# A two-layer decoder trunk in which an accumulating DMA, and no compute engine, forms the low halves of split weights

## The chip, the core and the metric

The kernel runs on one core of a Trainium2 chip. Its engines are TensorE (PE in the profile, with its weight loads as PEld), VectorE (DVE), ScalarE (ACT), GpSimd (POOL) and SyncE (SP), which here only issues DMAs. SBUF is the core's working memory, PSUM takes the matmuls' results, and 16 DMA engines move data between DRAM and SBUF or within SBUF. The metric is the device time of one execution in microseconds (us), as the median of several runs.

## What is computed

A sequence of 16 meta tokens and 512 real ones passes through differential attention, a feed-forward network (FFN), an attention in which every query keeps only its best keys, and a second FFN. All arithmetic is float32. The parts that matter here are the products with weights:

```python
def conv_ffn(h, w_up, conv_w, conv_b, w_down):
    u = h @ w_up
    ...
    return (jax.nn.silu(g) * val) @ w_down

q, k, v = jnp.split(h @ w_qkv, 3, axis=-1)          # layer 0
...
return o.reshape(B, T, DA_HEADS * 2 * DA_HEAD_DIM) @ w_o
q, k, v, qi, ki, wi = jnp.split(h @ w_in, DSA_SPLITS, axis=-1)   # layer 1
...
return o.reshape(B, T, DSA_QKV) @ w_o
```

## The kernel before, in words

Each float32 operand of a matmul is split into a rounded high part and a low part that holds the rest, both in the type float32r. A product is then three matmuls: high by high, high by low, low by high. Activations lie in SBUF, feature by token, 528 tokens wide (512 or 516 in the last layer's FFN).

Weights come in *slabs*: 1024 rows (896 for the first two thirds of the FFN's second matrix) by 128 columns, as one tile of 128 partitions by 1024 (896) float32, 512 (448) KB. The list `slabs` holds all 211 in the order of their use. For each, `loader` takes one of three tiles `raw` and SP issues the load. `splitter` takes a pair of tiles (high `wh`, low `wl`) from the buffer `WH` and emits `parts`, which fills the pair; then `raw` returns to the loader. `project` emits the slab's matmuls, 48 for a full slab (8 row blocks, 3 products, 2 spans of tokens), and returns the pair.

`WH` owns two pairs. While the attention's key tiles `K` are idle, `lend_keys` lends `WH` two more pairs made of them: from the end of layer 0's attention through the first FFN, and again from the end of layer 1's attention to the end of the kernel. `keys_back` reclaims them when the first normalised block of layer 1's input is ready, a few slabs before the first FFN ends. So the profile names a pair's high part `wh` or `K` and its low part `wl` or `K`.

`parts` has two forms. Slabs of queries, keys and index queries (`perm=True`, 36 of them) are split in two halves with permuted columns, and one odd slab has its own form. The other 174 pass `two(...)` on the whole tile: ACT casts the high part, then DVE or POOL subtracts. These are 88 slabs of the FFNs' up matrices, 54 of the down matrices (32 of them 448 KB), 8 value slabs and 8 output slabs in layer 0, and the same in layer 1. The first two slabs of the list have `on = (v,)`; both are `perm` slabs.

The order of instructions is not written by hand. Every step is an `Op` that a `Plan` emits: a list scheduler with a clock for each engine and a cost for each operation (`Op._cost`). Among tasks that are ready it emits the earliest, and the task of lower number at a near tie. For an `Alt` (several engines could do it) it takes the engine that ends first, with a bias against DVE. A DMA costs its queue 1016 ns on POOL or 560 ns on SP in that table and makes its result late by its size; each engine then executes what stands in its queue strictly in order.

The last layer's FFN ends with twelve half steps: the last twelve slabs are six weight blocks, each loaded twice, once for the first 256 tokens and once for the last 256 (24 matmuls each), so that the first half can be normalised, turned and written out while the second is computed.

The lines that the change's steps touch:

```python
yield Alt([e.copy(hi, src) if e is s else e.tensor_copy(out=hi, in_=src) for e in hi_on])
yield Alt([e.tensor_tensor(out=lo, in0=src, in1=hi.bitcast(F32), op=ALU.subtract) for e in on])
```

(in `two`; `s` is ACT, `v` DVE, `g` POOL, `sy` SP) and

```python
w = yield WH
yield from parts(loaded[i], *w)
RAW.put(loaded[i])
```

(in `splitter`). A copy of a key tile's two halves of partitions, `g.dma_start(out=K[b:b + 64, :, :], in_=K[a:a + 64, :, :])` in `k_stack`, is the only DMA on POOL's queue before.

Of the kernel before, what the change touches and what calls it, by code (L numbers as in the profile page):

```python
# [13 lines left out]
ALU = mybir.AluOpType  # L14
# [308 lines left out]
def hybrid_trunk(ctx: ExitStack, tc: tile.TileContext, A, out):  # L323
    nc = tc.nc
    plan = Plan(tc)
    v, s, g, pe, sy = (Engine(n, e) for n, e in (
        ("dve", nc.vector), ("act", nc.scalar), ("pool", nc.gpsimd), ("pe", nc.tensor), ("sp", nc.sync)))
# [64 lines left out]
    def two(hi, lo, src, scale=None, on=(v,), hi_on=(s,)):  # L392

        if scale is None:
            yield Alt([e.copy(hi, src) if e is s else e.tensor_copy(out=hi, in_=src) for e in hi_on])
            yield Alt([e.tensor_tensor(out=lo, in0=src, in1=hi.bitcast(F32), op=ALU.subtract) for e in on])
        else:
            yield s.mul(hi, src, scale)
            yield v.scalar_tensor_tensor(out=lo, in0=src, scalar=scale, in1=hi.bitcast(F32),
                                         op0=ALU.mult, op1=ALU.subtract)  # L400

    def mm(o, lhsT, rhs, start, stop):
        return pe.matmul(o, lhsT, rhs, start=start, stop=stop)

# [9 lines left out]
    def slab(load, parts):  # L414
        slabs.append((load, parts))
        ld.append(Event())
        sp_.append(Event())
        return len(slabs) - 1

    def plain(src, nk, perm=False):  # L420
        n = nk * P

        def load(raw):
            yield sy.dma_start(out=raw[:, :n].rearrange("p (k c) -> p k c", c=P), in_=src)

        on = (g, v) if len(slabs) > 1 else (v,)

        def parts(raw, wh, wl):
            if not perm:
                yield from two(wh[:, :n], wl[:, :n], raw[:, :n], on=on)  # L430
                return

            ri = raw[:, :n].rearrange("p (c h g i) -> p g c h i", h=2, g=2, i=16)
            vh = wh[:, :n].rearrange("p (c g h i) -> p g c h i", h=2, g=2, i=16)
            vl = wl[:, :n].rearrange("p (c g h i) -> p g c h i", h=2, g=2, i=16)
            for i in range(2):
                yield from two(vh[:, i], vl[:, i], ri[:, i], on=on)
        return slab(load, parts)
# [24 lines left out]
    def project(ps, w, xh, xl, nk, spans, M=P, ld=P, ev=None):  # L463

        wh, wl = w
        first = 512 - (spans[0][1] - spans[0][0]) if len(spans) == 2 else 0
        for k in range(nk):
            if ev is not None:
                yield ev[k]
            yield [mm(ps[:M, (512 if i else first):][:, :b - a], ww[:, k * ld:k * ld + M], x[k][:, a:b],  # L470
                      k == 0 and j == 0, k == nk - 1 and j == 2)
                   for j, (ww, x) in enumerate(((wh, xh), (wh, xl), (wl, xh)))
                   for i, (a, b) in enumerate(spans)]
        WH.put(w)
# [119 lines left out]
    def scores(X, K, first, use, prio):  # L594

        def one(o, b, c0, c1):
            return [mm(o, X[:, BLK[b][0]:BLK[b][1]], K[:, i, c0:c1], i == 0, i == 1) for i in range(2)]

        ends = []

        def used(views, t):
            left = Event(len(views))

            def free():
                left.set()
                if left.n == 0:
                    SC.put(t)
            for b, view in views:
                ends.append(spawn(use(b, view, free), prio))

        t = yield SC
        yield one(t[:, SP0:512], 4, 0, CUT) + one(t[:, 512:SP0 + T], 4, CUT, T)
        used([(4, t[:, SP0:SP0 + T])], t)
        t = yield SC
        yield one(t[:, :400], 3, 0, 400) + one(t[:, 512:784], 2, 0, 272)
        used([(3, t[:, :400]), (2, t[:, 512:784])], t)
        t = yield SC
        yield one(t[:, :256], 1, 0, 256) + (one(t[:16, 512:768], 0, 0, 256) if first else [])
        used([(1, t[:, :144])] + ([(0, t[:16, 512:528])] if first else []), t)
        return ends  # L620
# [47 lines left out]
    def values(po, passes, z, zt, ends):  # L668

        first = True  # L670
        for i, js in enumerate(((1, 2), (3, 4))):
            yield ends[i]
            for st, mv in passes:
                ops = []
                for j in js:
                    o, w = PJ[j]
                    ops.append(mm(po[:, 1024 - w:], st(j), mv[:, o:o + w], first, False))
                    first = False
                yield ops
        yield [mm(po[:, TP0:512], z, zt[:, :16], True, True), mm(po[:, 512:], z, zt[:, 16:], False, True)]  # L680
# [839 lines left out]
```

## Time and profile before

| what | value |
|---|---|
| median of 3 runs | 1418.88 us (1417.88 to 1421.92) |
| profiled execution, its own time | 1417.88 us |
| its span, first to last instruction | 1416.1 us |
| PE busy | 1372.6 us, 97% |
| DVE busy | 960.7 us, 68% |
| ACT busy | 679.9 us, 48% |
| POOL busy | 347.5 us, 25% |
| moved by DMA | 124.33 MB, mean 88 GB/s |

The page's second part cuts the span into 40 slices: PE stands at 9 tenths or more in nearly all, DMA between 1 and 4 tenths after the start. All operations are recorded through one helper, so every row has line L270 and a group is told by its tiles. In the rows, `ps` is a PSUM tile, `R` the split activations, `ident` the matrix for transposes, `tt`, `ns`, `st` scratch; `x2` behind a shape is a count. Times in a timeline are microseconds from the span's start.

### The profile page before, as it was taken

Reading aid. Unit: us, or ns where it says so; the run is one execution under the profiler, and the core shown is the slowest. Engines: PE = TensorE matmul, PEld = TensorE weight load, DVE = VectorE, ACT = ScalarE, POOL = GpSimd, SP = SyncE. Lnnn points to the kernel's source line nnn. Section 1 sums busy time; section 2 is a strip of 40 time slices with the busy share of each in tenths; the row PEclk is TensorE's granted clock in tenths of the full one; section 3 lists DMA queues with packets and bytes.
Section 4 is the critical chain, followed back from the end, with each engine's and each line's share of the span. In section 5 each row is a group of like instructions: output and inputs, shape, how many; then the busy total and the mean of one; then the engine's idle time right before and its main releaser. Section 6 shows DMA issues by size and latency. Waiting matters only on the chain. (4 is left out here: it accounts for less than half of the span.)

```text
span 1416.1 us, 26368 instructions
## 1 busy us (share of the span) xinstructions
PE 1372.6 (97%) x10703; PEld 1331.9 (94%) x10703; DVE 960.7 (68%) x1659; ACT 679.9 (48%) x1260; POOL 347.5 (25%) x441
## 2 busy tenths in 40 slices
PE   8989999999999999999989989999999999999997
PEld 7888999999999999999989989898999989989997
DVE  6878767457645763775599988887666637646764
ACT  4566676434423432443356477777444324423454
POOL 1654654420000000000247764442310000000012
PEclk8999999999999999999999999999999999999999
DMA  6422233233233323332312331222333233333333
GB/s 178 103 61 61 76 91 103 57 96 90 81 95 94 87 82 102 90 90 70 90 45 75 83 96 49 69 68 76 94 90 97 80 104 92 91 101 90 90 113 111
DMA packets 223084, 124.33 MB, mean 88 GB/s; under 512 B 7001, under 2 KB 218338, under 8 KB 222962
## 3 DMA queue, kind: packets, MB, share of 16 engines
q1 hardware_dynamic: 219234, 111.89, 27.5%
q0 software_dynamic: 2560, 8.65, 2.9%
q10 hardware_dynamic: 1168, 2.10, 0.4%
q8 instruction: 84, 1.38, 0.4%
q14 instruction: 38, 0.31, 0.1%
HBM read 111.87 MB, written 2.10 MB: 80 GB/s over the span
## 5 line engine op out<-in xcount | busy, mean ns | idle before, releaser
L270 PE MATMUL ps<-R,wh 128*128 128x256 f32 (+4 forms) x4016 | 680.8, 289 | 1.6 <-POOL R L270 0.9
L270 PEld LDWEIGHTS ps<-R,wh 128*128 128x128 f32 (+1 forms) x4016 | 562.5, 189 | 9.4 <-POOL R L270 1.1
L270 PE MATMUL ps<-R,wl 128*128 128x272 f32 (+3 forms) x2008 | 424.4, 288 | 0.0
L270 PE MATMUL ps<-R,K 128*128 128x256 f32 (+3 forms) x3240 | 418.4, 289 | 0.0
L270 PEld LDWEIGHTS ps<-R,K 128*128 128x128 f32 x3240 | 405.6, 189 | 7.6
L270 PEld LDWEIGHTS ps<-R,wl 128*128 128x128 f32 x2008 | 312.2, 188 | 3.2
L270 ACT CAST wh<-raw 128x1024 fp32r<-128x1024 f32 (+3 forms) x173 | 145.6, 847 | 202.7 <-PE ps L270 147.6
L270 DVE TENSOR_TENSOR wl<-raw,wh 128x1024 fp32r<-128x1024 f32 (+3 forms) x128 | 139.9, 1096 | 23.6 <-ACT wh L270 21.8
L270 DVE TENSOR_TENSOR h<-ps,h 128x528 f32<-128x528 f32 (+3 forms) x70 | 45.7, 653 | 143.0 <-PE ps L270 143.0
L270 DVE TENSOR_TENSOR tt<-ps,rbc 128x528 f32<-128x528 f32 (+2 forms) x89 | 62.4, 701 | 114.9 <-PE ps L270 109.6
L270 DVE SCALAR_TENSOR_TENSOR tt<-tt,cw,tt 128x528 f32<-128x528 f32 (+1 forms) x176 | 133.4, 758 | 8.2 <-ACT tt L270 4.9
L270 ACT CAST K<-raw 128x1024 fp32r<-128x1024 f32 (+1 forms) x76 | 77.9, 1027 | 119.9 <-PE ps L270 105.5
L270 POOL TENSOR_TENSOR acc<-acc,tt 128x528 f32<-128x528 f32 (+1 forms) x22 | 36.2, 1645 | 400.6 <-ACT tt L270 400.6
L270 ACT CAST R<-tt 128x512 fp32r<-128x512 f32 (+2 forms) x84 | 48.5, 585 | 139.7 <-DVE tt L270 139.6
L270 DVE TENSOR_TENSOR K<-raw,K 128x1024 fp32r<-128x1024 f32 (+1 forms) x75 | 89.6, 1195 | 10.8 <-ACT K L270 9.3
L270 PE MATMUL ps<-K,X 128*128 128x272 f32 (+2 forms) x464 | 79.7, 308 | 11.0 <-DVE tt L270 5.6
L270 ACT ACTIVATE ns<-ns,st 128x528 f32<-128x528 f32 (+4 forms) x160 | 82.1, 514 | 13.6 <-DVE st L270 11.8
L270 POOL TENSOR_TENSOR wl<-raw,wh 128x512 fp32r<-128x512 f32 (+1 forms) x45 | 70.4, 1566 | 47.6 <-ACT wh L270 47.0
L270 PEld LDWEIGHTS ps<-K,X 128*128 128x128 f32 x464 | 65.6, 182 | 15.9 <-DVE st L270 3.9
L270 ACT ACTIVATE tt<-tt,cw 128x528 f32<-128x528 f32 (+1 forms) x88 | 72.3, 821 | 14.8 <-DVE tt L270 14.6
L270 POOL MEMSET tt<- 128x2 f32 x44 | 4.2, 99 | 302.2 <-DVE tt L270 302.2
L270 ACT ACTIVATE tt<-tt 128x528 f32<-128x528 f32 (+1 forms) x44 | 28.1, 639 | 81.8 <-DVE tt L270 81.7
(120 smaller groups left out, 1359.0 us busy)
## 6 DMA issues: line engine op xcount, KB each, us to landing
raw<-in_ffn_w_up_dram SPq DMA_DIRECT2D x88, 512.0 KB
raw<-in_ffn_w_down_dram SPq DMA_DIRECT2D x32, 448.0 KB
raw<-in_dsa_w_in_dram SPq DMA_DIRECT2D x28, 512.0 KB
raw<-in_da_w_qkv_dram SPq DMA_DIRECT2D x24, 512.0 KB
raw<-in_ffn_w_down_dram SPq DMA_DIRECT2D x22, 512.0 KB
K<-K POOLq DMA_DIRECT2D x32, 264.0 KB, 3.0
raw<-in_da_w_o_dram SPq DMA_DIRECT2D x8, 512.0 KB
raw<-in_dsa_w_o_dram SPq DMA_DIRECT2D x8, 512.0 KB
```

The lines of the kernel that those rows point to most:

```text
L270: self.tc.keep_in_program_order(op.call(*op.a, **op.k))
```

## The change

The slabs whose columns are not permuted no longer pass `two` but a new function `low`. ACT writes the rounded slab as before. ACT then writes the negated, rounded slab into the low tile, and a DMA on POOL's queue adds the raw slab to it in place. The subtraction on DVE or POOL is gone for these 174 slabs. The permuted slabs and the activations keep `two`.

```diff
+    def low(hi, lo, src):
+
+        yield s.copy(hi, src)
+        yield s.mul(lo, src, -1.0)
+        yield g.dma_start(out=lo, in_=src, accum_op=ALU.add)
+
...
         def parts(raw, wh, wl):
             if not perm:
-                yield from two(wh[:, :n], wl[:, :n], raw[:, :n], on=on)
+                if len(on) > 1:
+                    yield from low(wh[:, :n], wl[:, :n], raw[:, :n])
+                else:
+                    yield from two(wh[:, :n], wl[:, :n], raw[:, :n], on=on)
                 return
```

Since the scheduler sees other operations, it also orders the rest anew. Three places matter below.

On POOL, in layer 1 before the selection of keys, where value slabs are split one after the other (`wl` is the low part, `R` a split value block, `zv` values of the meta tokens). Before:

```order
L270 TENSOR_TENSOR wl_115<-raw_111,wh_114 128x1024
L270 TENSOR_TENSOR tt_108<-tt_108 16x128
L270 COPY zv<-tt_108 16x128 x4
L270 TENSOR_TENSOR wl_117<-raw_112,wh_116 128x1024
L270 TENSOR_TENSOR R_87<-tt_105,R_87 128x4x64
L270 TENSOR_TENSOR R_88<-tt_105,R_88 128x4x64
```

After, in the same place:

```order
L270 DMA wl_117<-raw_111 128x1024
L270 TENSOR_TENSOR R_100<-tt_101,R_100 128x4x64
L270 TENSOR_TENSOR R_71<-tt_101,R_71 128x4x64
L270 DMA wl_115<-raw_112 128x1024
L270 TENSOR_TENSOR tt_105<-tt_105 16x128
L270 COPY zv<-tt_105 16x128
```

The subtraction on POOL has become an issue of a DMA that waits in POOL's queue for ACT's negated copy.

On SP, at the very end of its queue (loads of the last slabs, then the output rows):

```order
 L270 DMA raw_113<-in_ffn_w_down_dram 128x8x128
-L270 DMA raw_111<-in_ffn_w_down_dram 128x8x128
 L270 DMA out_dram<-ns_126 128x512 x2
-L270 DMA out_dram<-ns_128 128x512 x2
-L1516 UNCONDITIONAL_BRANCH
+L270 DMA raw_111<-in_ffn_w_down_dram 128x8x128
+L270 DMA out_dram<-ns_126 128x512 x2
+L1525 UNCONDITIONAL_BRANCH
```

The last weight load now stands behind two output DMAs, which wait for DVE's scaled rows of the first half.

On ACT, in the same twelve half steps (`h` is the residual stream, squared and scaled for the last norm). Before:

```order
L270 CAST K_123<-raw_111 128x1024
L270 ACTIVATE tt_108<-h_67 128x256
L270 ACTIVATE h_67<-h_67,gcol 128x256
L270 CAST K_122<-raw_112 128x1024
L270 ACTIVATE tt_105<-h_68 128x256
L270 ACTIVATE h_68<-h_68,gcol 128x256
```

After:

```order
L270 CAST wh_114<-raw_112 128x1024
L270 ACTIVATE wl_115<-raw_112 128x1024
L270 ACTIVATE tt_104<-h_67 128x256
L270 ACTIVATE h_67<-h_67,gcol 128x256
L270 CAST wh_116<-raw_113 128x1024
L270 ACTIVATE wl_117<-raw_113 128x1024
```

Each slab now puts two full-tile passes into ACT's queue, ahead of the residual's work.

## Rows read from the trace of the kernel before

**Rows 1.** The page's part 1: busy time, share and instructions of each engine.

```profile
PE 1372.6 (97%) x10703; PEld 1331.9 (94%) x10703; DVE 960.7 (68%) x1659; ACT 679.9 (48%) x1260; POOL 347.5 (25%) x441
```

**Rows 2.** Windows: length, busy PE, PEld, DVE, ACT, POOL; clock, DMA share, GB/s.

```profile
280.00:650.00 370.00, 370.00 (x3040) 369.98 (x3040) 222.66 (x270) 136.75 (x166) 16.42 (x55) 1.00 0.32 93
700.00:760.00 60.00, 55.76 (x418) 54.53 (x417) 55.18 (x98) 33.77 (x80) 32.95 (x32) 0.94 0.19 54
760.00:820.00 60.00, 56.85 (x453) 56.22 (x452) 59.76 (x176) 30.21 (x70) 47.79 (x63) 0.97 0.34 89
...
1060.00:1360.00 300.00, 300.00 (x2198) 284.96 (x2197) 183.03 (x226) 108.92 (x133) 0.00 (x0) 1.00 0.32 94
```

**Rows 3.** Groups by shape, slab splitting: busy us, mean ns, idle before, releaser.

```profile
L270 ACT CAST wh<-raw 128x1024 fp32r<-128x1024 f32 x82 | 86.1, 1050 | 135.0 <-PE ps L270 101.0 <-issue 33.8
...
L270 DVE TENSOR_TENSOR wl<-raw,wh 128x1024 fp32r<-128x1024 f32 x74 | 92.0, 1243 | 16.2 <-ACT wh L270 15.2
...
L270 POOL TENSOR_TENSOR wl<-raw,wh 128x1024 fp32r<-128x1024 f32 x8 | 19.5, 2436 | 5.0 <-ACT wh L270 4.9
```

**Rows 4.** DMA queues (packets, MB, share of 16 engines); issues (KB, us to landing).

```profile
q1 hardware_dynamic: 219234, 111.89, 27.5%
q0 software_dynamic: 2560, 8.65, 2.9%
...
K<-K POOLq DMA_DIRECT2D x32, 264.0 KB, 3.0
```

**Rows 5.** Group by shape: POOL's own time for issuing those copies.

```profile
L270 POOL DMA_DIRECT2D K<-K x32 | 18.1, 566 | 22.5 <-DVE K L270 17.9 <-POOL K L270 3.0 <-DVE st L270 1.0
```

**Rows 6.** Timeline of ACT in the first FFN: start, us, idle before, releaser.

```profile
446.98 1.05 ACT L270 CAST K<-raw 128x1024 fp32r<-128x1024 f32 x1 [1.41 <-PE ps L270]
...
452.85 1.05 ACT L270 CAST K<-raw 128x1024 fp32r<-128x1024 f32 x1 [0.67 <-PE ps L270]
```

**Rows 7.** Timeline of ACT where the first FFN ends and layer 1 begins.

```profile
663.25 1.05 ACT L270 CAST wh<-raw 128x1024 fp32r<-128x1024 f32 x1 [3.63 <-issue]
...
669.07 1.05 ACT L270 CAST wh<-raw 128x1024 fp32r<-128x1024 f32 x1 [3.60 <-issue]
```

**Rows 8.** Timelines of ACT, POOL, PE at layer 0's first two value slabs.

```profile
38.10 1.05 ACT L270 CAST wh<-raw 128x1024 fp32r<-128x1024 f32 x1 [3.61 <-PE ps L270]
...
43.94 0.65 PE L270 MATMUL ps<-R,wh 128*128 128x272 f32 x4
...
63.61 1.03 ACT L270 CAST wh<-raw 128x1024 fp32r<-128x1024 f32 x1
...
64.72 2.71 POOL L270 TENSOR_TENSOR wl<-raw,wh 128x1024 fp32r<-128x1024 f32 x1
...
68.10 0.65 PE L270 MATMUL ps<-R,wh 128*128 128x272 f32 x4
```

**Rows 9.** Timelines of ACT, PE and SP in the twelve half steps.

```profile
1378.58 1.05 ACT L270 CAST wh<-raw 128x1024 fp32r<-128x1024 f32 x1 [0.91 <-PE ps L270]
...
1381.39 1.05 ACT L270 CAST wh<-raw 128x1024 fp32r<-128x1024 f32 x1 [0.89 <-PE ps L270]
...
1395.13 1.06 ACT L270 CAST wh<-raw 128x1024 fp32r<-128x1024 f32 x1 [0.81 <-PE ps L270]
...
1403.51 0.40 PE L270 MATMUL ps<-R,wh 128*128 128x256 f32 x2
...
1344.10 42.83 SPq L270 DMA_DIRECT2D raw<-in_ffn_w_down_dram  x11
1393.37 1.55 SPq L270 DMA_DIRECT2D out_dram<-ns  x2
```

**Rows 10.** Timelines of ACT and POOL at layer 1's value slabs.

```profile
755.63 1.05 ACT L270 CAST wh<-raw 128x1024 fp32r<-128x1024 f32 x1 [1.68 <-PE ps L270]
762.09 1.05 ACT L270 CAST wh<-raw 128x1024 fp32r<-128x1024 f32 x1 [1.42 <-PE ps L270]
...
764.79 2.40 POOL L270 TENSOR_TENSOR wl<-raw,wh 128x1024 fp32r<-128x1024 f32 x1
```

## The prediction, made before the changed kernel ran

> **What bounds the kernel now.** I read the page's busy shares first: PE works 97% of the span, DVE 68%, ACT 48%, POOL 25% [rows 1]. An average over stages hides where the rest lies, so I read windows next [rows 2]. In the first FFN's 370 us and in 300 us of the second, PE is busy to the last digit; DVE there is at about 60%. What leaves DVE in those stages can gain nothing, and they hold 142 of the 174 slabs that change. All that any change of this kind can win is PE's idle time, 1416.1 - 1372.6 = 43.5 us over the whole span. The one stage in which DVE sets the pace is layer 1's selection of keys (59.76 of 60 us in 760 to 820).
>
> So the question is how late the low halves may come. A slab's cast on ACT waits for PE to return a pair (PE is the releaser in [rows 6]), so the time from that cast to the slab's first matmul is the cover. With four pairs it is three slabs of PE work, with two pairs one slab.
>
> **What leaves and what comes, per slab.** Before, a split is one cast (1.05 us) and one subtraction: 1.24 us on DVE or 2.44 on POOL [rows 3], 2.3 us together in the usual case. After, ACT makes two passes; the second has the cast's size, so 1.05 us again, 174 times at most 1.05 = 183 us more on ACT, which spends 137 of 370 us in the first FFN [rows 2] and has room. DVE loses 165 subtractions, POOL 9.
>
> The accumulating DMA is not in the trace. Two rows bound it [rows 4]. The weight loads (queue q1) took 27.5% of 16 engines for 111.89 MB: 0.275 x 16 x 1416.1 / 111.89 = 55.7 engine-us per MB, so 1.82 us of all 16 engines for a slab of 0.524 MB. The copies of K within SBUF (q0) took 2.9% for 8.65 MB: 76 engine-us per MB, 2.49 us for a slab. An add must read the raw slab and the low tile and write the low tile. At the cheapest it is one pass at the loads' rate, 1.82 us; at the dearest two passes at the copy's rate, 4.98. The copy of K runs from one half of the partitions to the other, while a slab lies on all 128 like a load, so I stand nearer to the loads' row and take two passes at its rate, 3.64 us.
>
> Latency: a K copy of 264 KB lands 3.0 us after issue [rows 4], of which 264/512 x 2.49 = 1.28 is movement; 1.72 is fixed. Its issue costs POOL 0.57 us for 64 partitions [rows 5]; I add the same for 128. Issue to landing is then 1.72 + 0.57 + 3.64 = 5.9 us. With two ACT passes and 0.2 us of hops, **a split takes 8.2 us instead of 2.3**; 5.8 with the cheap DMA (3.54), 11.4 with the dear one queued behind a load (9.1).
>
> Collectives: The Full Stack, in the Trainium skill (section "The bandwidth ceiling: the fold count and why AG ≠ RS ≠ AR"), says that an add in the DMA path is slower than a copy because of its two source reads, not because of the arithmetic. Worked out from its 31 GB/s per engine, halved, a slab would take about 2.1 us, an estimate from that page; no run here shows it yet.
>
> **The FFNs, 0 us.** A slab's period is 370 / 3040 x 48 = 5.84 us [rows 2]; casts stand 5.87 apart [rows 6]. Four pairs give 17.5 us of cover: enough at 5.8, 8.2 and 11.4. A raw tile is held for the split and a load of some 3 to 4 us (by the K copy's landing), under 12.5 of 17.5 us. The 16 DMA engines carry 1.82 + 3.64 = 5.46 us per 5.84. That hides it, narrowly; if this cover is gone, every slab pays (first rival).
>
> **The seam, +4.8 us.** Where layer 1's norm takes the key tiles back, three slabs run on two pairs: casts at 663.25, at 669.07 [rows 7] and one more at the same distance, 5.82 us. A split of 8.2 us is 2.4 late. A late slab also delays PE's return of its pair, so every second slab pays: 2 x 2.4 = 4.8, from 0 (5.8) to 11 (11.4).
>
> **Layer 0, +5 us.** Of its first two value slabs, one is cast at 38.10 and used at 43.94, the other at 63.61 and 68.10 [rows 8]: 5.84 and 4.49 us of cover, short by 2.4 and 3.7. In the new PE order 20 score matmuls stand ahead of such a slab's end, so I take 5 of 6.1, from 0 to 11. Later slabs there have 8 us or more.
>
> **Layer 1's values, 0.** Casts 6.46 us apart [rows 10], so a split is 1.8 late on every second of about five slabs: 2 x 1.8 = +3.6. Against that, DVE loses three subtractions in the stage that it bounds: 3 x 1.24 = -3.7. From -3.7 to +6. POOL's queue holds value splits and copies behind each waiting DMA (the new order shows it); POOL had 32.95 of 60 us busy there.
>
> **The end, +7 us.** In the twelve half steps casts come 2.81 us apart [rows 9], half the usual period, so a raw tile has 8.4 us between its slabs. A split of 8.2 and a load of 3.4 to 5 need 11.6 to 13.2. Counted slab by slab from the first short step, the raw tiles fall 2.5 us behind on the third reuse, 6 to 8 on the seventh. Besides, SP's last load now stands behind two output DMAs that before were issued at 1393.37, while the last load had gone out by 1344.10 + 42.83 = 1386.9 [rows 9]. Issued at 1393.4 plus the 3 us by which the first half is late, landed 4 later and split 8.2 later, the last slab is ready at 1408.6; before, cast at 1395.13, PE reached it at 1403.5 [rows 9]. So 5 to 8 us: 7, from 1.4 (5.8) to 20.
>
> **Clock, +2.** In 700 to 760, with 4.2 us of PE idle, the mean granted clock is 0.94 [rows 2]: 0.06 x 60 = 3.6 us of lost full clock. A few new stalls of 2 to 4 us bring perhaps one such drop; 0 to 7.
>
> **Sum.** 4.8 + 5 + 0 + 7 + 2 = 18.8 on a span of 1416.1: 1434.9. The profiled execution lies 1.8 above its span (1417.88) and 1.0 under the median, so I forecast **1438 us**. With all bounds at their lowest (0 + 0 - 3.7 + 1.4 + 0) it is 1417, at their highest (11 + 11 + 6 + 20 + 7) 1474.
>
> **Rival 1: the DMA engines become the bound.** If the add costs two passes at the K copy's rate, a slab needs 1.82 + 4.98 = 6.80 us of the engines, against 5.84 in the first FFN and 5.71 (516 columns) in the second; 448 KB slabs need 5.95 against 5.11 and 4.96. That is 52 x 0.96 + 46 x 1.09 + 16 x 0.84 + 16 x 0.99 = 129 us, and 12 x (6.80 - 2.82) = 48 in the half steps instead of 7; with 6 more in the other places, 1438 + 129 + 41 + 6 = 1614. It decides from 5.84 - 1.82 = 4.02 us per add on, and there PE would stall in every slab. For it: the K copy is the only transfer within SBUF that the trace has. Against it: that copy uses half of the partitions at each end. The rule of the Trainium skill's page Collectives: The Full Stack (same section), that two reads halve the rate, gives just this when it is put on the copy's row.
>
> **Rival 2: faster.** If the add lands within 3.5 us of its issue, a split is no longer than the 5.8 us of cover with two pairs, and nothing stalls but the end (1.4). Then the stage that DVE bounds decides: three subtractions less there (-3.7), and POOL, rid of four at 2.4 us [rows 10], could take other work from DVE, at most 4 x 2.4 at POOL's double price, -4.8. 1418.9 + 1.4 - 8.5 = 1412. Against it: even the cheap DMA is only just that fast.
>
> **Rival 3: no difference.** The scheduler counted a DMA's latency when it set the order, so scores and transposes may fill each late split; only the end's 1.4 us and the lost DVE time are left: 1417 to 1420.
>
> That the change does not do what it says is unlikely: all 174 DMAs stand in POOL's order.
>
> **Chances.** My forecast 0.52, rival 1 0.28, rival 3 0.12, rival 2 0.08. A measurement of this kernel can tell about 0.3%, 4.3 us, from no change. The lower edge of my own case adds 0.02 to "same": faster 0.08, same 0.14, slower 0.78. The range goes from 1412 to rival 1's 1614, beyond which half of that rival (0.14) lies, and below it about 0.05; the forecast's own is 1417 to 1474.
>
> **What would show it.** Right: PE still without idle time in 280 to 650; POOL's adds landing 5 to 7 us after issue; casts 2.4 us or more later than PE wants them at the seam; the last load issued after the output DMAs. Wrong: PE idle in each FFN slab with a releaser "DMA" (rival 1), or the DMA share near 1 in the FFNs; or PE's idle sum below 43.5 us (rival 2). The forecast falls first with the price of one add: under 2 us it is too high, over 4 far too low.

## The result: 45 us slower, and not where the sum had put it

| what | before | after |
|---|---|---|
| median of the runs | 1418.6 us | 1463.8 us (1460.34 to 1466.18) |
| ratio | | 1.0312, 95% interval 1.0284 to 1.034 |
| profiled execution's span | 1416.1 us | 1464.4 us |
| PE busy | 1372.6 us | 1387.0 us |

The forecast was 1438. The direction is right and the time lies in the range, but the change costs 45 us where the forecast put 19. Of the span's 48.3 us, PE's idle time makes 33.9 (43.5 to 77.4) and its busy time 14.4: the same 10703 matmuls took longer. The page of the kernel after (part 1; part 3, queues: packets, MB, share of 16 engines; part 6, issues: count, KB, median us to landing) stands against [rows 1, 4]:

```profile
PE 1387.0 (95%) x10703; PEld 1341.5 (92%) x10703; DVE 758.5 (52%) x1502; ACT 836.2 (57%) x1432; POOL 447.7 (31%) x600
...
q0 software_dynamic: 27616, 97.79, 38.1%
q1 hardware_dynamic: 219234, 111.89, 27.0%
...
wl<-raw POOLq DMA_DIRECT2D x81, 512.0 KB, 5.6
K<-raw POOLq DMA_DIRECT2D x61, 512.0 KB, 6.5
```

DVE lost 202 us, ACT gained 156, POOL 100. The price of an add can now be read: q0 took 0.381 x 16 x 1464.4 = 8927 engine-us; without the K copies' 8.65 MB at 76 that is 8270 for 89.1 MB, 92.8 engine-us per MB, so 3.04 us of all 16 engines for a slab. It lands 5.6 to 6.5 us after its issue. The same work by shape, from the groups of the kernel after (busy us, mean ns, idle before, releaser):

```profile
L270 ACT ACTIVATE wl<-raw 128x1024 fp32r<-128x1024 f32 x81 | 85.3, 1053 | 0.0
L270 ACT CAST wh<-raw 128x1024 fp32r<-128x1024 f32 x81 | 84.9, 1048 | 81.0 <-PE ps L270 65.2 <-issue 8.5 <-DMA raw<-in_ffn_w_down_dram 5.1
L270 POOL DMA_DIRECT2D wl<-raw x97 | 84.2, 869 | 366.6 <-ACT wl L270 331.2 <-ACT tt L270 26.2 <-DMA raw<-in_ffn_w_down_dram 4.7
```

The second pass costs 1.05 us as the cast does. POOL stands 331 us in front of adds whose negated slab ACT has not written yet, which costs nothing where four pairs stand ready, as the FFNs' windows show next.

Windows of the kernel after (length; busy PE, PEld, DVE, ACT, POOL; clock, DMA share, GB/s), against [rows 2]:

```profile
280.00:650.00 370.00, 370.00 (x3040) 369.98 (x3040) 148.06 (x205) 198.62 (x236) 71.97 (x120) 1.00 0.86 183
760.00:820.00 60.00, 58.23 (x475) 57.53 (x473) 59.87 (x187) 33.62 (x80) 37.55 (x65) 1.00 0.44 106
1060.00:1380.00 320.00, 320.00 (x2363) 305.28 (x2363) 130.19 (x183) 170.75 (x203) 50.48 (x60) 1.00 0.88 185
1380.00:1465.00 85.00, 61.68 (x421) 57.94 (x420) 22.83 (x44) 41.29 (x63) 12.12 (x16) 0.90 0.73 169
```

Both FFNs still run without a gap, at a DMA share of 0.86 and 0.88. DVE still bounds the selection of keys (59.87 of 60). The half steps are broken: PE is busy for 61.68 of 85 us, at a granted clock of 0.90. PE's waits (us in total, times, longest) name the adds first:

```profile
PE ps L270 <- DMA wl<-raw: 16.6, 10, 5.2
PE ps L270 <- DMA K<-raw: 10.0, 3, 4.7
PE ps L270 <- DVE st L270: 6.1, 6, 1.8
PE ps L270 <- DVE ns L270: 4.5, 7, 1.0
PE ps L270 <- POOL acc L270: 4.1, 1, 4.1
```

This list misleads, as the experiments show: in layer 0 the waits for `wl` are not what the kernel pays for.

**Where along the kernel the time goes** shows when each of the 211 slabs begins on PE. In the table stands the start of the slab's first matmul minus that in the trace before, in us, from the PE timelines of the profiled executions (number 139, for example: 1040.8 before, 1067.7 after). The columns on the right are experiments, told below. Differences below 2.5 us appear between traces that are alike at that place.

| slab: place | after | FFNs only | attention only | half steps only | old order with adds | new order, no adds | old order, no adds in half steps, sums on DVE | fourth raw tile |
|---|---|---|---|---|---|---|---|---|
| 32: first FFN begins | 9.8 | -1.9 | 9.8 | -1.3 | -2.1 | 14.8 | 0.3 | 11.0 |
| 60: inside it | 9.6 | -1.9 | 9.7 | -1.3 | 4.4 | 14.7 | 2.5 | 10.9 |
| 96: near its end | 9.5 | -2.0 | 9.6 | -1.3 | 4.4 | 14.5 | 2.4 | 10.7 |
| 101: layer 1 has begun | 10.8 | 0.1 | 9.6 | -1.3 | 7.7 | 14.5 | 5.8 | 11.8 |
| 127: last key slab | 14.1 | 1.0 | 11.5 | 0.4 | 12.0 | 17.5 | 10.5 | 15.8 |
| 137: second FFN's first slab | 20.4 | 1.0 | 17.8 | 0.4 | 14.3 | 20.8 | 12.7 | 22.1 |
| 139: its third | 26.9 | 1.0 | 18.3 | 0.4 | 20.8 | 20.8 | 17.8 | 22.0 |
| 198: last before the half steps | 26.7 | 1.0 | 18.2 | 0.4 | 20.8 | 20.7 | 17.8 | 21.9 |
| 210: last slab | 40.5 | 1.0 | 18.4 | 16.7 | 38.0 | 20.5 | 17.5 | 33.2 |
| end of the span | 48.3 | 1.0 | 18.6 | 17.4 | 38.2 | 20.5 | 17.7 | 33.4 |

The column "after" reads: layer 0 +9.8, first FFN 0, into layer 1 +1.3, layer 1 +9.6, the second FFN's first two slabs +6.5, the rest of it 0, the half steps and what follows +21.6. For this last part, windows from the first matmul of slab 199 to the end of the span, before and after:

```profile
1370.00:1416.10 46.10, 38.44 (x325) 37.69 (x323) 22.97 (x33) 23.85 (x41) 14.66 (x13) 0.95 0.39 123
1396.80:1464.40 67.60, 44.88 (x325) 43.34 (x324) 15.76 (x34) 31.14 (x49) 9.57 (x13) 0.88 0.70 164
```

PE's idle time grows there by 15.1 us (7.7 to 22.7) and its busy time by 6.4 for the same 325 matmuls, at a mean granted clock of 0.88 instead of 0.95.

### The profile page after: what moved, and what is told of

The parts are those of the page before. It is cut to its first block, busy times and chain, and to the rows that moved or that the text cites. A ratio compares the mean times of both kernels' runs of the same rounds, so it can differ in the third digit from the quotient of the medians.

```text
span 1464.4 us, 26757 instructions
## 1 busy us (share of the span) xinstructions
PE 1387.0 (95%) x10703; PEld 1341.5 (92%) x10703; DVE 758.5 (52%) x1502; ACT 836.2 (57%) x1432; POOL 447.7 (31%) x600
## 4 chain that ended last, share of the span: by engine, by line
PE 64%; DVE 12%; issue 8%; DMA 5%; ACT 5%; POOL 4%; SPq 0%; POOLq 0%; ACTq 0%; DVEq 0%
PE ps L270 64%; DVE tt L270 4%; DVE acc L270 3%; POOL tt L270 2%; DVE st L270 2%; DMA wl<-raw 2%; DVE ns L270 1%; DMA raw<-in_ffn_w_down_dram 1%; ACT ns L270 1%; ACT tt L270 1%; DMA K<-raw 1%; ACT K L270 1%; DVE wl L270 1%; DVE X L270 1%; ACT wh L270 1%
## 5 line engine op out<-in xcount | busy, mean ns | idle before, releaser
L270 PE MATMUL ps<-R,wh 128*128 128x256 f32 (+3 forms) x3984 | 679.5, 291 | 0.0
L270 PEld LDWEIGHTS ps<-R,wh 128*128 128x128 f32 x3984 | 561.8, 190 | 7.4 <-DVE R L270 0.2
L270 PE MATMUL ps<-R,K 128*128 128x272 f32 (+3 forms) x3288 | 431.4, 291 | 13.0 <-DMA K<-raw 10.0
L270 PE MATMUL ps<-R,wl 128*128 128x272 f32 (+4 forms) x1992 | 425.5, 290 | 17.5 <-DMA wl<-raw 16.6
L270 PEld LDWEIGHTS ps<-R,K 128*128 128x128 f32 x3288 | 416.2, 190 | 21.9 <-DMA K<-raw 10.6
L270 PEld LDWEIGHTS ps<-R,wl 128*128 128x128 f32 (+1 forms) x1992 | 312.5, 190 | 23.3 <-DMA wl<-raw 19.0
L270 POOL DMA_DIRECT2D wl<-raw x97 | 84.2, 869 | 366.6 <-ACT wl L270 331.2
L270 POOL DMA_DIRECT2D K<-raw x77 | 66.2, 859 | 337.7 <-ACT K L270 320.0
L270 ACT ACTIVATE wl<-raw 128x1024 fp32r<-128x1024 f32 (+1 forms) x97 | 100.5, 1036 | 0.0
L270 ACT ACTIVATE ns<-ns,st 128x528 f32<-128x528 f32 (+4 forms) x160 | 82.0, 514 | 18.3 <-DVE st L270 17.5
L270 ACT ACTIVATE K<-raw 128x1024 fp32r<-128x1024 f32 (+1 forms) x77 | 79.4, 1031 | 0.0
L270 POOL TENSOR_TENSOR wl<-raw,wh 128x512 fp32r<-128x512 f32 (+1 forms) x40 | 52.7, 1319 | 51.0 <-ACT wh L270 47.3
```

The lines of the kernel that those rows point to most:

```text
L270: self.tc.keep_in_program_order(op.call(*op.a, **op.k))
```

## Experiments

### Which places: FFNs, attention layers, half steps

Theory P: the loss sits at a few places. Rival D: it is spread over all adds by their traffic or the clock. Three kernels change some slabs only; here with `i_` as the slab's number:

```diff
-                if len(on) > 1:
+                if 32 <= i_ < 100 or 137 <= i_ < 199:                    # FFNs
+                if len(on) > 1 and (i_ < 32 or 100 < i_ < 137):          # attention
+                if i_ >= 199:                                            # half steps
                     yield from low(wh[:, :n], wl[:, :n], raw[:, :n])
```

> Only the FFNs' slabs (130 of the 174; not the twelve half steps) get their low half from the adding DMA; the other 44 keep the subtraction. Theory P (places): the change costs nothing where four pairs stand ready, and its 45 us are lost at a few places outside, so this kernel takes 1419 to 1425 us; up to 6 of it may come at the end of layer 1, where the second FFN's first slabs are split. PE is busy to the last digit in the middle of both FFNs. Rival D (traffic): the adds, some 73 MB of them here, cost in proportion by their load on the DMA engines or on the clock: 130/174 x 45 = 34 us, so about 1452.

Measured: 1420.1 us, ratio 1.0011 (1.0001 to 1.002). The windows of this kernel:

```profile
280.00:650.00 370.00, 370.00 (x3042) 369.98 (x3041) 148.02 (x205) 194.72 (x230) 69.92 (x120) 1.00 0.85 180
1060.00:1360.00 300.00, 300.00 (x2202) 285.15 (x2201) 122.63 (x172) 156.98 (x188) 46.51 (x54) 1.00 0.87 185
```

130 of the 174 adds cost nothing that counts: PE has no gap and the clock stays at 1.00 with the DMA engines 85% busy. Rival D falls.

> Only the 32 slabs of values and output projections in the two attention layers get their low half from the adding DMA; the FFNs and the half steps keep the subtraction. Theory P: in the trace after, the slabs run 9.7 us late by the end of layer 0, 4.4 more through layer 1's values and selection, and 12.8 more by the start of the second FFN; if these slabs alone cause that, it is 27 us, 1445; if the second FFN's first slabs have a part in the 12.8, 1432 to 1445. Rival D: 32/174 x 45 = 8 us, 1427.

Measured: 1437.0, ratio 1.0133 (1.0116 to 1.0149). 32 slabs cost 18.7 us: 9.8 in layer 0 and 8 in layer 1. The second FFN's start costs 0.5 here, and 0 with the FFNs alone; its 6.5 need both sets of adds.

> Only the twelve half steps' slabs get their low half from the adding DMA. Theory P: in the trace after, the slabs of the half steps fall 13.8 us further behind and the end some 8 more; so +14 to +21 us, 1433 to 1440, with PE waiting for the adding DMAs there and the last load behind two output DMAs. Rival D: 12/174 x 45 = 3 us, 1422. My prediction's term for this place was +7, 1426.

Measured: 1436.8, ratio 1.0131 (1.0113 to 1.015). Twelve slabs cost 18.5 us. The three parts add up to 1.8 + 18.7 + 18.5 = 39 of the 45 us; the 6 left are the second FFN's start.

### Late low halves, or another order

In the attention layers two things changed at once: the low half comes later, and the scheduler, which counts other costs, deals all instructions anew. Four kernels take them apart. The first two keep the new order: one puts a subtraction on DVE at the add's place, the other leaves the add out.

```diff
         yield s.copy(hi, src)
-        yield s.mul(lo, src, -1.0)
-        yield g.dma_start(out=lo, in_=src, accum_op=ALU.add)
+        yield put_for(s.mul(lo, src, -1.0))
+        yield put_for(g.dma_start(out=lo, in_=src, accum_op=ALU.add),
+                      v.tensor_tensor(out=lo, in0=src, in1=hi.bitcast(F32), op=ALU.subtract))
```

(`put_for(a, b...)` lets the scheduler count `a` and issues `b...` in its place, or nothing.)

> The order of all instructions is that of the changed kernel, but the low half is again one subtraction, on DVE, at the place where POOL issued the adding DMA; the negated pass on ACT is gone. Theory L (lateness): the 45 us come from low halves that arrive late, so in the same order with early low halves the kernel is back at 1419 to 1428. Rival O (order): the scheduler, which sees a longer split, puts the rest in a worse order, and that is the loss; then this kernel stays at 1445 or above. Both in part would give 1430 to 1445.

Measured: 1454.2, ratio 1.0253 (1.0238 to 1.0269). The half steps lose nothing (36.1 us late at both ends), but layer 0 is 28 us late. The total lies where rival O put it, but the loss in layer 0 is more than with the adds, so this run has a fault of its own: the scheduler doesn't count these subtractions, and DVE has more to do than it thinks. It settles the half steps, not layer 0. The next kernel has no such load:

```diff
-        yield g.dma_start(out=lo, in_=src, accum_op=ALU.add)
+        yield put_for(g.dma_start(out=lo, in_=src, accum_op=ALU.add))
```

> The order of all instructions is that of the changed kernel, with both ACT passes, but the adding DMA is left out: the low tile keeps the negated slab (so the low parts are not the reference's), ready some 2 us after the cast. DVE and POOL are not loaded as in the run with the subtraction. Theory L: with early low halves the changed kernel's order costs little, 1418 to 1425. Rival O: the order itself costs the 18 us of the attention layers and 6 at the start of the second FFN, so 1437 to 1444, with no loss in the half steps.

Measured: 1437.0, ratio 1.0127 (1.0109 to 1.0144), the low edge of rival O: **the order alone costs 18.6 us**, all of it in the attention layers (14.8 and 6), nothing in the half steps. (ACT's second pass is still in this kernel; the next run has it too, in the old order.) PE's waits over the whole kernel:

```profile
PE ps L277 <- DVE ns L277: 10.6, 14, 1.3
PE ps L277 <- DVE st L277: 3.8, 5, 2.0
PE ps L277 <- DVE tt L277: 3.2, 7, 0.8
```

No wait for an add is left; in its place PE waits for the softmax's scratch rows (`ns`), 10.6 us instead of 4.5. So the 6.2 us that PE waited for `wl` in layer 0 of the kernel after were not 6 us to be won: without the adds other waits stand in their place. The counterpart keeps the old order and issues the new work:

```diff
-        yield s.mul(lo, src, -1.0)
-        yield g.dma_start(out=lo, in_=src, accum_op=ALU.add)
+        yield Alt([put_for(e.tensor_tensor(out=lo, in0=src, in1=hi.bitcast(F32), op=ALU.subtract),
+                           s.mul(lo, src, -1.0), g.dma_start(out=lo, in_=src, accum_op=ALU.add))
+                   for e in (g, v)])
```

> The scheduler still sees one cast and one subtraction for each slab and so puts out the order of the kernel before; what is issued in the subtraction's place is the negated pass on ACT and the adding DMA. Theory L: the loss in the attention layers (18 us there, and 6 where layer 1 meets the second FFN) is that the low half arrives late for a fixed order; an order that doesn't know of it then loses at least as much: 1455 to 1480 with the 18 us of the half steps. Rival O: the loss in the attention layers is the new order; then only the half steps' 18 us are left, 1435 to 1440.

Measured: 1454.6, ratio 1.0259 (1.0226 to 1.0291), against 1463.8 (1.0284 to 1.034) in the new order: a scheduler that doesn't know of the adds does no worse than one that does, and by the medians better. **In layer 0 late low halves cost nothing** (-2.1 us at slab 32). They cost 3.3 where layer 1 begins, 6.6 more to the second FFN, and 6.5 at the start of each FFN. PE's waits over the whole kernel:

```profile
PE ps L277 <- POOL acc L277: 10.3, 3, 4.9
PE ps L277 <- DMA wl<-raw: 10.1, 8, 2.7
PE ps L277 <- DMA K<-raw: 7.8, 3, 4.7
```

Layer 0 can be split into PE's idle and busy time. These are windows from the span's start to the first matmul of slab 32, with the same 2148 matmuls in each: before; after; new order without adds; old order with adds.

```profile
0.00:299.70 299.70, 279.94 (x2148) 268.08 (x2149) 213.59 (x458) 171.62 (x392) 150.03 (x179) 0.97 0.35 92
0.00:309.50 309.50, 282.62 (x2148) 269.24 (x2149) 181.62 (x439) 189.73 (x410) 153.80 (x198) 0.99 0.49 116
0.00:314.50 314.50, 288.43 (x2148) 273.98 (x2149) 184.07 (x439) 190.00 (x410) 137.94 (x179) 0.95 0.32 88
0.00:297.60 297.60, 278.69 (x2148) 266.78 (x2149) 192.96 (x444) 187.94 (x410) 149.25 (x193) 1.00 0.50 119
```

PE's idle time is 19.8, 26.9, 26.1 and 18.9 us. The new order costs 6 to 7 us of it, with the adds or without; the old order with the adds and both ACT passes costs none. The rest is busy time: in the run without adds the same matmuls took 8.5 us longer than before, so that it loses more in layer 0 than the kernel after. Some 7 of the 8.5 are the granted clock (0.05 x 314.5 - 0.03 x 299.7 = 6.7). (The clock was recorded only from 21 us on in the second and the fourth trace, so their 0.99 and 1.00 are not comparable.)

Neither theory holds alone. In layer 0 it is the order (O), in the half steps lateness (L); in layer 1, between slabs 101 and 137, the order alone costs 6.3 us, the late low halves alone 6.6, and both together 9.6.

Is the old order special? One more kernel has no adds; the scheduler counts ACT's full-slab passes 4% longer:

```diff
-            return n * 0.8333 + (51 if ...
+            return n * (0.8333 if n < 896 else 0.87) + (51 if ...
```

> The kernel before with no adding DMA at all; the scheduler counts ACT's passes over a whole slab 4% longer (984 ns instead of 946; the trace has 1027 to 1052), which changes its order in the attention layers and leaves the work as it is. Theory N (a tuned order): the order before is an especially good one, and any other that this scheduler makes loses about what the changed kernel's order lost: 5 to 18 us, 1424 to 1437. Rival S: the changed kernel's order is bad because of the long split; then this one costs nothing, 1416 to 1421.

Measured: 1424.4, ratio 1.0036 (1.0022 to 1.0049), the low edge of theory N. This one other order costs 5.7 us without any add, so a part of what the new order loses may come with any change of the order; 18.6 is more than that, but one such order does not show how far they spread. And if the scheduler is told the truth about the add?

```diff
-            self.late = 4e-3 * n * o.shape[0] / 0.36
+            self.late = 4e-3 * n * o.shape[0] / 0.36 + (2000.0 if self.k.get("accum_op") else 0.0)
```

> The changed kernel, but the scheduler counts each add 2 us longer, in traffic and in landing, so about 8 to 9 us for a split, as the trace shows it. Theory T (a wrong count): in the attention layers PE stood 6 us for adds that came later than counted; with the right count these go and the rest is the same: 1455 to 1460. Theory N (any new order loses or gains some 10 us there by chance): anywhere from 1450 to 1475, with the loss in other places of the attention layers. The half steps stay as they are in both.

Measured: 1460.2, ratio 1.0294 (1.0276 to 1.0312). The total would fit theory T, but its reason fails. PE's waits in layer 0 (40 to 315 us), the adds' in the kernel after first, then those of this kernel:

```profile
PE ps L270 <- DMA wl<-raw: 6.2, 6, 1.2
...
PE ps L270 <- DMA K<-K: 6.6, 2, 4.0
PE ps L270 <- POOL st L270: 4.2, 3, 2.9
PE ps L270 <- DMA wl<-raw: 1.9, 2, 1.1
...
PE ps L270 <- DMA K<-raw: 1.2, 1, 1.2
```

The waits for adds fell from 6.2 to 3.1 us (1.9 for `wl`, 1.2 for `K`), about as T said, and layer 0 still ends 9.0 us late, now with waits for key copies and POOL. The half steps lose 25.0 us instead of 21.6, where both theories had them unchanged. A part of the 10 to 15 us that the new orders cost layer 0 is busy time, as shown above; which trait of them makes PE wait longer stays open.

### The start of the second FFN

PE's wait there is for POOL's sum of squares (`acc`, 4.1 us). Theory Q: the additions stand in POOL's queue behind adds. So they go to DVE, in an unchanged order:

```diff
-                yield Alt([e.tensor_tensor(out=q, in0=q, in1=sq[:, cols], op=ALU.add) for e in (g, v)])
+                yield Alt([put_for(e.tensor_tensor(out=q, in0=q, in1=sq[:, cols], op=ALU.add),
+                                   v.tensor_tensor(out=q, in0=q, in1=sq[:, cols], op=ALU.add)) for e in (g, v)])
```

> The changed kernel in its own order, but every addition to the sum of squares that the scheduler gave to POOL runs on DVE. Theory Q (POOL's queue): at the start of the second FFN PE waits 4.1 us for POOL's sum (acc), because the sum's additions stand in POOL's queue behind adding DMAs that wait for their raw slab and for ACT; without them there, the 5.9 us lost between the slabs at the start of the second FFN go: 1457 to 1459. Rival: the norm is late for another reason (the residual itself, DVE); then 1462 to 1466.

Measured: 1462.1, ratio 1.0302 (1.0283 to 1.0321). The place loses 4.9 instead of 6.5 us, a difference within the 2.5 us above; POOL's queue is not the main cause. The same edit in the old order, without adds in the half steps:

> The order of the kernel before (the scheduler sees subtractions), adding DMAs for all slabs but the twelve half steps, and the sums of squares on DVE. Without these two edits that order gave 1454.6: of its span 6.5 us went at the start of each FFN, some 17 in the half steps with 5 behind them, and 10 within layer 1. Theory Q: both losses at the FFNs' starts go, and the half steps' as in the run with the adds there alone, so 1423 to 1430. Rival: the FFNs' starts stay late, 1435 to 1440.

Measured: 1434.4, ratio 1.011 (1.0095 to 1.0125), close to the rival: 5.1 us are lost at the second FFN's start; at the first's 2.2 instead of 6.5, so there POOL had a part. The end of ACT's timeline before the wait, in the kernel after (start, us, tile; idle before and releaser), shows what Q had missed:

```profile
1049.48 1.05 ACT L270 CAST K<-raw 128x1024 fp32r<-128x1024 f32 x1 [4.32 <-DMA raw<-in_ffn_w_up_dram]
1050.43 1.05 ACT L270 ACTIVATE K<-raw 128x1024 fp32r<-128x1024 f32 x1
1053.51 1.04 ACT L270 CAST K<-raw 128x1024 fp32r<-128x1024 f32 x1 [2.02 <-DMA raw<-in_ffn_w_up_dram]
1054.46 0.73 ACT L270 ACTIVATE R<-h,gcol 128x528 fp32r<-128x528 f32 x1
1055.09 0.63 ACT L270 ACTIVATE tt<-h 128x528 f32<-128x528 f32 x1
```

DVE had finished the last residual block (`h`) at 1049.54. ACT then stands before a cast whose raw slab has not landed, and the block's square (`tt<-h`) is behind it until 1055.09; the sum follows, and PE goes on at 1057.22. The raw slabs are late because their tiles were held by earlier adds: SP issued the two loads at 1042.04 and 1046.24, 4.6 and 5.7 us after POOL had issued the adds on those tiles (1037.49 and 1040.56). The loads themselves were slow too: 7.4 and 7.3 us from issue to the cast that waited for each, while in the trace before the last packet of a load at this place came 3.3 to 3.8 us after its issue. So a fourth raw tile, an idle scratch tile from the end of layer 1's attention on:

```diff
+        def lend_raw():
+            for e in e_o:
+                yield e
+            RAW.put((yield NS)[:, :1024])
+
+        spawn(lend_raw(), 2)
```

> The changed kernel with one idle scratch tile as a fourth raw tile from the end of layer 1's attention on, a slab before the second FFN. Theory A (ACT's queue behind the ring of raw tiles): at the start of the second FFN ACT stands 4.3 and 2.0 us for raw slabs that are late because their tile was held by an add, and the last block's square stands behind those casts in ACT's queue, so the sum comes late; a fourth tile takes most of the 5.9 us at this place away. In the half steps it takes some 7 us off, as it did with the adds there alone. Together 1449 to 1454. Rival: the place is late for another reason (DVE's residual, the new order as such); then only the half steps gain, 1455 to 1459.

Measured: 1451.1, ratio 1.022 (1.0203 to 1.0237), as theory A said: 22.1 us late before the place and 22.0 after it, and from slab 198 to the end of the span 11.5 us lost instead of 21.6. PE's first waits in 980 to 1070 us of this kernel no longer have `acc` among them:

```profile
PE ps L270 <- DMA wl<-raw: 2.8, 1, 2.8
PE ps L270 <- DVE pl L270: 2.2, 2, 1.8
```

The order differs here too (each square now stands behind one cast, not two), so the tile's share is not proven apart from that.

### The half steps: raw tiles, or the DMA engines

SP's timeline at the end of the kernel after (a row groups equal issues), then from POOL's and ACT's the add before and the cast behind the last load:

```profile
1400.23 25.15 SPq L270 DMA_DIRECT2D raw<-in_ffn_w_down_dram  x6
1427.03 1.34 SPq L270 DMA_DIRECT2D out_dram<-ns  x2
1433.79 0.39 SPq L270 DMA_DIRECT2D raw<-in_ffn_w_down_dram  x1
...
1427.52 0.92 POOL L270 DMA_DIRECT2D K<-raw  x1 [1.77 <-ACT K L270]
...
1442.80 1.05 ACT L270 CAST wh<-raw 128x1024 fp32r<-128x1024 f32 x1 [3.16 <-DMA raw<-in_ffn_w_down_dram]
```

Six loads in 25.15 us are 5.0 us apart, so a raw tile comes round every 15 us; PE wants a slab each 2.81. The last load does stand behind the output DMAs, but they had gone out by 1428.4; it waits for its tile, whose add POOL had issued at 1427.52, 6.3 us before. It then took 9.0 us to the cast that waited for it (1442.80); before, a load's last packet in the half steps came 3.4 to 3.8 us after its issue. So the ring is long in part because the DMA engines are busy, and the two theories that follow are not wholly apart. Theory R takes this ring as the bound, theory E the DMA engines, which need 4.86 us for each half step. Two kernels add raw tiles to the run with adds in the half steps alone (`RAW.put` of one scratch tile as above, or of two, with the output rows in other scratch tiles):

> As the run with the adds in the half steps alone (1436.8), but one idle scratch tile serves as a fourth raw tile from the end of layer 1's attention on. Theory R (ring of raw tiles): a raw tile is held for load, two passes and add, some 15 us, three tiles give a slab each 5 us where PE wants one each 2.81; with four it is 3.75, half of the loss goes: 1425 to 1428. Theory E (DMA engines): load and add need 1.82 + 3.04 = 4.86 us of 16 engines for each half step of 2.81, so another tile only brings one load forward, 1.8 us or so: 1433 to 1436.

Measured: 1429.4, ratio 1.0076 (1.0061 to 1.0091).

> As the run before, with two scratch tiles as fourth and fifth raw tile (the output rows then go through other scratch tiles). Theory R: five tiles give a slab each 3.0 us, next to no loss left: 1418 to 1423. Theory E: two loads come forward, 3.6 us: 1431 to 1435, with the DMA engines' share near 1 through the half steps.

Measured: 1430.1, ratio 1.0079 (1.0064 to 1.0094). The fourth tile takes back 7.4 us, the fifth nothing. Both times lie between the two theories' ranges, the first nearer to R's, the second nearer to E's. Windows with three raw tiles and twelve adds:

```profile
1370.00:1380.00 10.00, 10.00 (x84) 9.89 (x83) 3.57 (x8) 7.40 (x13) 1.68 (x2) 1.00 0.99 206
1380.00:1390.00 10.00, 5.30 (x43) 4.89 (x41) 2.12 (x5) 6.09 (x10) 1.68 (x2) 0.97 0.98 214
1390.00:1400.00 10.00, 9.22 (x58) 9.22 (x59) 1.27 (x3) 4.83 (x6) 1.62 (x3) 0.69 0.84 195
```

With five:

```profile
1370.00:1380.00 10.00, 10.00 (x88) 10.00 (x87) 3.70 (x9) 10.00 (x17) 2.52 (x3) 1.00 1.00 204
1380.00:1390.00 10.00, 7.63 (x60) 7.01 (x59) 2.13 (x5) 6.21 (x10) 2.54 (x3) 1.00 1.06 222
1390.00:1400.00 10.00, 3.62 (x24) 3.42 (x24) 0.85 (x2) 2.71 (x4) 0.85 (x1) 0.69 0.88 215
```

The DMA engines are full for 20 us in both. The granted clock falls to 0.69 (part of that stretch at 1.2 instead of 2.4 GHz) after PE was busy for 5.30 of 10 us, which makes the 9.22 busy us with three tiles worth less. With five tiles PE's longest wait in the half steps is not for an add (waits from 1362 us on):

```profile
ACT K L270 <- DMA raw<-in_ffn_w_down_dram: 8.7, 1, 8.7
...
PE ps L270 <- DVE acc L270: 6.4, 1, 6.4
```

The cast that ACT stands before, at 1396.48, is for a load issued at 1382.24, 14.2 us earlier. A square for the first half's norm stands behind it in ACT's queue, and DVE's sum (`acc`) waits for that square, as at the second FFN's start. The full engines act here through ACT's order; what they would cost without it is not shown. To load the engines less and leave the ring, every second half step got an add:

```diff
-                if i_ >= 199:
+                if i_ >= 199 and i_ % 2 == 0:
```

> Adding DMAs for every second slab of the twelve half steps alone (six adds), three raw tiles. Theory E (DMA engines): twelve loads and six adds are 12 x 1.82 + 6 x 3.04 = 40 us of 16 engines against 34 us of PE work and the lead of the first loads, so next to nothing is lost: 1418 to 1423. Theory R (ring of raw tiles): a raw tile is held some 9 us for a subtraction and 15 for an add, 12 on the mean, so three tiles give a slab each 4 us against 2.81, and nine slabs lose 1.2 us each: 1427 to 1431.

Measured: 1433.9, ratio 1.0101 (1.0086 to 1.0116). Its windows:

```profile
1370.00:1380.00 10.00, 10.00 (x86) 9.95 (x85) 4.59 (x9) 8.61 (x15) 2.79 (x3) 1.00 0.54 128
1380.00:1390.00 10.00, 7.67 (x66) 7.46 (x64) 3.08 (x7) 4.98 (x8) 0.86 (x1) 1.00 0.70 172
1390.00:1400.00 10.00, 8.82 (x77) 8.61 (x76) 5.61 (x11) 6.07 (x10) 2.67 (x3) 1.00 0.81 199
```

The engines have room, and most of the loss is still there, somewhat above what R gives. So the ring of three raw tiles binds first. Where it is widened, the time stops some 11 us above the kernel before, with the DMA engines full; that they, and not ACT's order, set this limit is likely but not shown.

No version here beats the kernel before. The adds are free only where four pairs stand ready, and what they relieve there, DVE, was not in the way.

## Why the prediction was wrong, step by step

Three of the four signs that the prediction named for being right appeared (PE without idle time in the first FFN, adds landing in 5 to 7 us, the last load behind the output DMAs), so they could not tell its mechanism from the real one. That the time lies in the forecast's own range, 1417 to 1474, is in part luck: layer 1 (9.6) and the end (21.6) lie above their highest values (6 and 20), one place had no term, and layer 0's 9.8 fits its range by another mechanism.

- **The FFNs, 0 us: right.** PE 370.00 of 370, with the adds alone there 1420.1. The add costs 3.04 us of the engines (3.64 taken, bounds 1.82 and 4.98), its issue to landing 5.6 to 6.5 us (5.9 taken; the cheap bound, 3.54, left out the 0.57 us of issue that the other two have, which changed nothing). Rival 1 decided from 4.02 and fell. The estimate from the Trainium skill's page Collectives: The Full Stack (section "The bandwidth ceiling: the fold count and why AG ≠ RS ≠ AR"), 2.1 us, was too low, and its rule put on the copy's row, 4.98, too high. An add cost 92.8 engine-us per MB against 76 for the K copy and 55.7 for a load: dearer than a copy, as the page says, but by 1.2 times where its two reads, by that page's rule for a ring of cores, would make it 2.
- **Layer 0, +5: the wrong mechanism, which is the main fault.** The term counted how late a low half is before a fixed row of matmuls. In the old order that costs nothing (-2.1), in the new order the loss is there without any add (14.8, of which 6.3 are PE's idle time and 8.5 busy time). The prediction had pieces of the new order before it and priced them at nothing: its sum had no term for the scheduler dealing the attention layers anew. That term is 18.6 us by the run without adds, the second largest of all.
- **The seam, +4.8: right for an order that stands still** (3.3 in the old order), but in the new one the casts there come earlier: the first FFN's end and the step into layer 1 cost 1.0 us in all.
- **Layer 1's values, 0: too low.** Layer 1 loses 9.6 us up to the second FFN, over its values, selection and output slabs together, of which the sum had the values alone; the order alone makes 6.3. The relief of DVE, -3.7, didn't show: DVE is still full in the selection (59.87 of 60).
- **The second FFN's start: not in the sum, 6.5 us.** The prediction looked at POOL's queue and at SP's, not at ACT's: its casts wait for raw slabs, and the residual's squares stand behind them. Its count that a raw tile is held "under 12.5 of 17.5 us" held in the FFN's even pace, not here, where the two loads took 7.3 and 7.4 us, counted at 3 to 4.
- **The end, +7: the right mechanism, mis-sized; 21.6 us.** The ring of raw tiles was counted at 11.6 to 13.2 us a round and took 15; its load was counted at 3.4 to 5 us and took 9.0 for the last slab. Missing beside it: the DMA engines need 4.86 us per half step of 2.81, which the prediction's own 1.82 + 3.64 would have shown, as it did for rival 1 only. The output DMAs ahead of the last load were not in the way.
- **Clock, +2: too low.** In the half steps alone the same matmuls kept PE busy 6.4 us longer, at a granted clock of 0.88. Over the whole kernel they took 14.4 us longer; how much of the other 8.0 the clock makes stays open.
- **Rivals 2 and 3 fell**: PE's idle sum rose from 43.5 to 77.4 us.

## What to carry to other kernels

Where a scheduler orders a kernel, a change of one operation's cost is two changes: price the work in the old order and the new order without the work, each by itself, and split each loss into PE's idle time and the busy time of the same matmuls. An accumulating DMA holds its source tile (the loads above went out 4.6 to 6.3 us after POOL had issued the add on their tile), so count the source's ring at the fastest pace that asks for it, and the DMA engines' time at that pace too, not at the mean. Look at what stands behind a waiting instruction on every queue, the one that feeds the transfer included.

## What the runs showed of the hardware

- An accumulating DMA within SBUF costs 92.8 engine-us per MB, 1.67 times a load from DRAM. Its median landing, 5.6 and 6.5 us in the kernel after, is 6.2, 8.3 and 8.5 in the three groups (two to four adds each) between 1375 and 1415 us of the run with four raw tiles, where the DMA engines are full.
- At a DMA share of 0.85 to 0.88 for hundreds of us PE loses neither time nor clock (1.00).
- Loads of 512 KB, whose last packet came 3.4 to 3.8 us after their issue in the half steps before (mean DMA share 0.39), took up to 9.0 us to the cast that waited for them beside the adds of the kernel after (0.70).
- The same 2148 matmuls of layer 0 kept PE busy for 279.9 us at a mean granted clock of 0.97 (before) and 288.4 us at 0.95 (new order without adds).
